# Matrix products without a reader, put at six waits of TensorE in a two-block network

## The chip, the cores and the metric

One core of a Trainium2 chip runs the whole program. Its engines are TensorE (PE, with its weight loads shown apart as PEld), VectorE (DVE), ScalarE (ACT), GpSimd (POOL) and SyncE (SP), which issues the DMAs here. The metric is the device time of one execution in microseconds (us); the time before is the median of three runs.

## The reference

A sequence of 256 tokens of width 1024 passes through four layers and then one more block, all in float32. Each of the four layers has a mixer (Mamba2, HGRN2, a gated delta net, Mamba2 again), a cross attention to 256 memory tokens with four heads, and a gated feed-forward net with a short convolution. The fifth block mixes an RWKV-7 recurrence with a differential attention and ends in a mixture of 32 experts. Cut to what matters here:

```
for i in range(4):
    x = x + mixer_i(rmsnorm(x, ln_mix[i]))            # i = 2: gated delta net
    s = q(x) @ k(mem).T * 256**-0.5                   # 4 heads
    x = x + (softmax(s) @ v(mem)) @ xa_o[i]
    x = x + glu_ffn(rmsnorm(x, ln_ffn[i]))
x = rmsnorm(x, final_norm)                            # passage to the second block
h = rms_norm(x, norm_mix)                             # "mixing"
x = x + (rwkv7(h) and diff_attention(h), gated) @ w_out
x = x + moe(rms_norm(x, norm_ffn))                    # router: top group, top 2 of 8 experts
```

The delta net solves unit triangular systems; the kernel inverts their 32 x 32 diagonal blocks (`base_inverse`) by some thirty steps on VectorE.

## The kernel before

Tokens are kept as two blocks `b` of 128 rows, `x[:, b]`. Every dense product is done in fp32r (a float32 form that PE takes in one pass) on operands split into a high and a low part: three products `l*xh + h*xl + h*xh` into the same PSUM tile (lines 327 to 329, 358 to 360, 395 to 397). ScalarE makes the high part of a weight piece (line 299), VectorE the low one (line 300). Products of plain float32 operands, such as the transposes against the identity (line 188) or against a scaled identity `dg` (line 190), appear in the trace as two records each.

PSUM has eight banks. Four belong to the pool `pm`, tag `m`: each tile of a dense product takes one in turn. The rest belong to a stage's pool `pa` and to the memory's keys and values.

A planner puts the instructions in order before the run. It goes through them with costs of its own and gives each engine the most urgent instruction whose operands are there by its reckoning; urgent is what comes earlier in the program text, and blocks in `high_priority(offset=n)` count as n places earlier. The result is one fixed order for each engine; an engine never steps past an instruction that waits.

The places that the change touches:

- *Begin.* `run` loads `x`, then tables; the tile of the identity and the ones, `id_ones` (trace name `m_ident`), is loaded in `consts`. The first work of PE is the first layer's `norm` (line 194): per token block, squares on ScalarE, `xns = x * gain` on VectorE (line 218), an inverse root by ten short VectorE operations, `dg` (line 234), and then the eight transposes of `transpose_split` (line 190).
- *Passage.* The same `norm`, called from `mix` with `first=final_norm`, does both norms in one; `kept` then holds the two roots of each block, and behind the transposes ScalarE scales `x` (line 237).
- *Last softmax.* `xattn` (line 548) runs for each token block: scores `s` (line 571) for two pairs of heads, maximum, exponentials with sums (line 588), division (line 593), transposes `tp` of the probabilities (line 598) and, after both blocks, the products `po` with the memory's values. `kT` holds the keys, split; `kTh` is its high part. The case `i == 3` is the last of the four.
- *Inverse.* `gdn` calls `base_inverse` (line 997), whose last act is two stream transposes of 128 x 1024 on VectorE (line 1013); the first gives `dT`. The next products of PE there are `pn` (line 1200).
- *Recurrence.* `mix` calls `diff_out` (line 1557): it scales the attention's output `od` by head (line 1563), transposes it (line 1564, `pod`) and splits it (lines 1566 and 1568); behind it stands the RWKV recurrence `wkv`, whose first products are `pA` (lines 1596 and 1597).
- *Router.* `moe` splits the scaled tokens into `hnh` and `hnl` (line 178) while VectorE works out the chosen experts; PE then counts places (`ppos`, lines 1820 to 1824), gathers tokens (`pxe`, line 1887) and starts the experts' first products (`pgu`, line 1917).

Of the kernel before, what the change touches and what calls it, by code (L numbers as in the profile page):

```python
# [11 lines left out]
F32 = mybir.dt.float32  # L12
# [37 lines left out]
class Net:  # L50
# [25 lines left out]
    def consts(self):  # L76
        i = np.arange(128)
        parts = {
            'ident': np.eye(128),
            'ones': np.ones((128, 128)),  # L80
            'neg': np.where(i[:, None] <= i[None, :], 0.0, -1e30),
            'bd32': i[:, None] // 32 == i[None, :] // 32,
            'sub32': np.concatenate([i[:, None] % 32 == i[None, :32],
                                     np.where(i[:, None] % 32 < i[None, :32], 0.0, -1e30),
                                     i[:, None] % 32 < i[None, :32],
                                     i[:, None] // 64 == i[None, :2], np.zeros((128, 30))], axis=1),
            'lin': (i[:, None] <= i[None, :]) * 1.0 - (i[:, None] < 64),
            'lst': (i[:, None] < i[None, :]) * 1.0 - (i[:, None] < 64),
            'blow': i[:, None] // 32 < i[None, :] // 32,
            'tri': i[:, None] <= i[None, :],  # L90
            'stri': i[:, None] < i[None, :],
            'mk3': i[:, None] <= i[None, :],
            'cz': np.zeros((128, 128)),
            'cneg': np.where(i[None, :] <= i[:, None], 0.0, -1e30),
            'tri32': (i[:, None] <= i[None, :]) & (i[:, None] // 32 == i[None, :] // 32),
        }
        self.parts = {k: np.asarray(v, np.float32) for k, v in parts.items()}
        self.c = {}
        self.masks('ident', 'ones', pool=self.const)
        self.ident = self.c['ident']  # L100

    def masks(self, *names, pool=None, **kw):
# [91 lines left out]
    def norm(self, gname, gain, first=None):  # L194
        nc = self.nc
        x = self.x
        g = self.row_table(gname, gain, pool=self.gpool, tag="gain")
        if first is not None:
            gf = self.wpool.tile([128, PIECE], F32, name="wt")[:, :D]
            self.row_load(gf, "final_norm", first)  # L200
        xns = self.wpool.tile([128, 2, D], F32, name="wt")
        hl = self.split_tiles("xn")
        kept = []
        with self.tc.high_priority(offset=NORM):
            for b in range(2):
                xn = xns[:, b]
                ss = self.spool.tile([128, 2, 2], F32, name="ss")
                for n in range(2):
                    s = slice(n * 512, n * 512 + 512)
                    xs = x[:, b, s]  # L210
                    junk = hl[1][:, 4 * n:4 * n + 4, b * 128:b * 128 + 128]
                    sq = lambda k: nc.scalar.activation(junk, xs.rearrange("p (k t) -> p k t", k=4), AF.Square,
                                                        accum_out=ss[:, k, n:n + 1])
                    sq(0)
                    if first is not None:
                        nc.vector.tensor_tensor(xs, xs, gf[:, s], ALU.mult)
                        sq(1)
                    nc.vector.tensor_tensor(xn[:, s], xs, g[:, s], ALU.mult)
                if first is None:
                    m = self.spool.tile([128, 1], F32, name="ssm")  # L220
                    nc.vector.tensor_tensor(m, ss[:, 0, 0:1], ss[:, 0, 1:2], ALU.add)
                    r = self.ms_rsqrt(m, D)
                else:
                    m = self.spool.tile([128, 2], F32, name="ssf")
                    r2 = self.spool.tile([128, 2], F32, name="rsf")
                    nc.vector.tensor_tensor(m, ss[:, :, 0], ss[:, :, 1], ALU.add)
                    nc.vector.tensor_scalar(m, m, KAPPA / D, None, op0=ALU.mult)
                    nc.vector.tensor_scalar(m[:, 0:1], m[:, 0:1], KAPPA * EPS, None, op0=ALU.add)
                    nc.vector.scalar_tensor_tensor(m[:, 1:2], m[:, 0:1], EPS, m[:, 1:2], op0=ALU.mult, op1=ALU.add)
                    self.rsqrt(r2, m)  # L230
                    kept.append(r2)
                    r = r2[:, 1:2]
                dg = self.spool.tile([128, 128], F32, name="dg", bufs=2)
                nc.vector.tensor_scalar(dg, self.ident, r, None, op0=ALU.mult)
                self.transpose_split(hl, xn, b, KD, dg=dg)
        for b, r2 in enumerate(kept):
            nc.scalar.activation(x[:, b], x[:, b], AF.Copy, scale=r2[:, 0:1])
        self.rb = None
        return hl
# [132 lines left out]
    def linear_K(self, src, name, w, kc, tag="ahl", bufs=2):  # L372
        nc = self.nc
        ap = self.dram("in_" + name, pack(w, D))
        ps = [[self.pm.tile([128, 512], F32, name=f"pK{b}{n}", tag="m") for n in range(2)] for b in range(2)]
        for q in range(0, kc, 2):
            ws = self.weights(ap[0][:, q * D:(q + 2) * D], 2 * D)
            if isinstance(tag, str):
                t = self.apool.tile([128, 2, 2, T], F32R, name="ahl", tag=tag, bufs=bufs)
                hl = t[:, 0], t[:, 1]  # L380
            else:
                hl = [self.apool.tile([128, 2, T], F32R, name="ahl", tag=x, bufs=bufs) for x in tag]
            self.split(hl, slice(None), src(q) if callable(src) else src[:, q:q + 2])
            xh, xl = hl
            end = q + 2 == kc
            order = [(k, b, n) for k in range(2) for b in range(2) for n in range(2)]
            if end:
                order.sort(key=lambda x: (x[2], x[1]))
            for k, b, n in order:
                h, l = ws[k]  # L390
                first, last = q + k == 0, q + k == kc - 1
                bs = slice(b * 128, b * 128 + 128)
                c = slice(n * 512, n * 512 + 512)
                p = ps[b][n]
                nc.tensor.matmul(p, xh[:, k, bs], l[:, c], start=first, stop=False)  # L395
                nc.tensor.matmul(p, xl[:, k, bs], h[:, c], start=False, stop=False)  # L396
                self.last_mm = nc.tensor.matmul(p, xh[:, k, bs], h[:, c], start=False, stop=last)  # L397
                if last:
                    self.residual(n, b, p)

    def linear_T(self, *a, **k):
        for f in self.tiles_T(*a, **k):
# [145 lines left out]
    def xattn(self, i):  # L548
# [8 lines left out]
        kT, qT = self.split_tiles("kT", pool=self.apool), self.split_tiles("qT", pool=self.apool)  # L557
# [15 lines left out]
        for b in range(2):  # L573
# [4 lines left out]
            for g in range(2):  # L578
                s = self.pa.tile([128, 2, T], F32, name="s", tag="a")
                for j in range(2):  # L580
                    h = 2 * g + j
# [4 lines left out]
                for j in range(2):  # L586
                    h = 2 * g + j
                    nc.scalar.activation(pr[:, h], s[:, j], AF.Exp, bias=mx[:, h:h + 1], scale=rs[:, b:b + 1],
                                         accum_out=sm[:, h:h + 1])
            rc = self.spool.tile([128, 4], F32, name="rc")  # L590
            nc.vector.reciprocal(rc, sm)
            for h in range(4):
# [8 lines left out]
        for h in range(4):  # L601
            p = self.pa.tile([128, 2, T], F32, name="po", tag="a")
# [34 lines left out]
    def run(self, out):  # L637
        self.x = self.xpool.tile([128, 2, D], F32, name="x")
        ax = self.dram("in_x", self.data['x'].reshape(T, D)).rearrange("(b p) d -> p b d", p=128)
        with self.tc.high_priority(offset=4 * LOAD):  # L640
            for b in range(2):
                self.load(self.x[:, b], ax[:, b])
        self.out = out.rearrange("(b p) d -> p b d", p=128)
        first = [s for s in STAGES if s[:-1] not in ('mix', 'moe')]
        if first:
            self.first_block(first)
# [387 lines left out]
    def gdn(self, i):  # L1034
        nc, d, c = self.nc, self.data, self.c
        w = d['g_in_w'][0]
# [84 lines left out]
        for b in range(2):  # L1121
# [6 lines left out]
            for h in range(8):  # L1128
                for q in range(4):
# [7 lines left out]
                                    pk[:, :, None, :].to_broadcast([128, 8, 2, 32]), ALU.mult)  # L1137
        dT, dD = [x.rearrange("p (b h) i -> p b h i", b=2)
                  for x in self.base_inverse(md.rearrange("p b h i -> p (b h) i"), "inv", 2, reuse=True, xtag="vtok")]
        for b in range(2):  # L1140
            nc.vector.tensor_tensor(dD[:, b], dD[:, b], nb[:, b, :, None].to_broadcast([128, NH, 32]), ALU.mult)
        qT = unit("qT_", 0, 128 ** -0.5)
# [159 lines left out]
    def mix(self, i):  # L1302
# [254 lines left out]
        def diff_out():  # L1557
            odT = [late("odT", [128, 4, T], F32R, tag="o", bufs=2) for _ in range(2)]
            r = self.ms_rsqrt(dss, 128)
            for b in range(2):  # L1560
# [6 lines left out]
                for h in range(4):  # L1567
                    nc.vector.scalar_tensor_tensor(odT[1][:, h, t], pt[:, h], sub[:, 0:1], odT[0][:, h, t].bitcast(F32),
                                                   op0=ALU.mult, op1=ALU.subtract)
            return odT  # L1570


# [185 lines left out]
    def moe(self, i):  # L1758
# [84 lines left out]
        for n in range(2):  # L1843
            for b in range(2):
                self.split_scaled((hnh, hnl), (slice(None), b, slice(n * 512, n * 512 + 512)), parts[b][n], self.r[:, b:b + 1])

        slots = ['xw'] * XW + ['wt'] * 4 + ['hl'] * 3 + ['xnh', 'xnl']
        count = [0]
# [221 lines left out]
```

## Time and profile before

| | |
|---|---|
| median of three runs | 2945.12 us (2937.13 to 2953.91) |
| profiled execution | 2940.76 us, span 2939.0 us |
| mean granted clock of PE | 0.988 |
| busy: PE, DVE, ACT | 2816.4, 1884.7, 1534.5 us |
| DMA | 599.47 MB, mean 204 GB/s |

The span runs from the first instruction to the last; all instants below are counted from its start. The granted clock is 1.00 at 2.4 GHz and 0.50 at 1.2 GHz. Matmuls overlap, so the duration of one is longer than the distance to the next; a pace is read from a count and the time that it took. A line of idle time in brackets says how long the engine stood still before the group, and what released it.

### The profile page before, as it was taken

Reading aid. Unit: us, or ns where it says so; the run is one execution under the profiler, and the core shown is the slowest. Engines: PE = TensorE matmul, PEld = TensorE weight load, DVE = VectorE, ACT = ScalarE, POOL = GpSimd, SP = SyncE. Lnnn points to the kernel's source line nnn. Section 1 sums busy time; section 2 is a strip of 40 time slices with the busy share of each in tenths; the row PEclk is TensorE's granted clock in tenths of the full one; section 3 lists DMA queues with packets and bytes.
Section 4 is the critical chain, followed back from the end, with each engine's and each line's share of the span. In section 5 each row is a group of like instructions: output and inputs, shape, how many; then the busy total and the mean of one; then the engine's idle time right before and its main releaser. Section 6 shows DMA issues by size and latency. Waiting matters only on the chain.

```text
span 2939.0 us, 47392 instructions
## 1 busy us (share of the span) xinstructions
PE 2816.4 (96%) x18834; PEld 2344.3 (80%) x18834; DVE 1884.7 (64%) x3690; ACT 1534.5 (52%) x2870; POOL 5.4 (0%) x19
## 2 busy tenths in 40 slices
PE   8999899999999998999999999989989999999998
PEld 7998899887899897888898999879878785433334
DVE  7886578667678679677786788658769673111103
ACT  7785555555655466675555687545554533111113
POOL 0000000000000000000000000000000000000000
PEclk9999999999999999999999999999999999999999
DMA  5444455552655453235455444535544249999996
GB/s 212 151 158 172 152 197 200 179 189 102 199 187 196 155 179 123 97 120 180 166 200 184 167 150 141 191 122 191 195 155 158 73 178 372 423 422 424 422 423 252
DMA packets 119029, 599.47 MB, mean 204 GB/s; under 512 B 20624, under 2 KB 26769, under 8 KB 56977
## 3 DMA queue, kind: packets, MB, share of 16 engines
q1 hardware_dynamic: 118800, 596.37, 55.1%
q8 instruction: 150, 2.46, 0.3%
q14 instruction: 79, 0.64, 0.1%
HBM read 586.89 MB, written 9.44 MB: 203 GB/s over the span
## 4 chain that ended last, share of the span: by engine, by line
PE 78%; DVE 9%; ACT 7%; DMA 4%; issue 2%; SPq 0%; ACTq 0%; DVEq 0%
PE pT L327 9%; PE pT L329 9%; PE pT L328 9%; PE pgu L1917 7%; PE pK L395 4%; PE pK L396 4%; PE pK L397 4%; PE pM L358 4%; PE pM L359 4%; PE pM L360 4%; PE pyd L1963 3%; PE pkv L538 3%; DVE wl L300 2%; ACT wh L299 1%; DMA kw<-in_xa_v 1%
## 5 line engine op out<-in xcount | busy, mean ns | idle before, releaser
L300 DVE TENSOR_TENSOR wl<-wt,wh 128x1024 fp32r<-128x1024 f32 x620 | 756.4, 1222 | 332.9 <-ACT wh L299 331.7
L299 ACT ACTIVATE wh<-wt 128x1024 fp32r<-128x1024 f32 x620 | 656.3, 1062 | 488.4 <-PE pT L329 234.1
L327 PE MATMUL pT<-xnh,wl 128*128 128x256 f32 x2672 | 746.5, 280 | 4.2 <-DVE wl L300 3.5
L328 PE MATMUL pT<-xnl,wh 128*128 128x256 f32 x2672 | 745.7, 279 | 0.7 <-DVE xnl L174 0.7
L329 PE MATMUL pT<-xnh,wh 128*128 128x256 f32 x2672 | 745.9, 279 | 0.0
L327 PEld LDWEIGHTS pT<-xnh,wl 128*128 128x128 f32 x2672 | 503.5, 189 | 9.0 <-DVE wl L300 5.7
L328 PEld LDWEIGHTS pT<-xnl,wh 128*128 128x128 f32 x2672 | 503.6, 188 | 2.1 <-DVE xnl L174 1.3
L329 PEld LDWEIGHTS pT<-xnh,wh 128*128 128x128 f32 x2672 | 503.8, 189 | 1.9 <-issue 1.3
L396 PE MATMUL pK<-wh,ahl 128*128 128x512 f32 x576 | 230.0, 399 | 0.3 <-DVE ahl L174 0.3
L395 PE MATMUL pK<-wl,ahl 128*128 128x512 f32 x576 | 228.3, 400 | 1.4 <-DVE wl L300 1.0
L397 PE MATMUL pK<-wh,ahl 128*128 128x512 f32 x576 | 229.1, 398 | 0.0
L358 PE MATMUL pM<-wl,xnh 128*128 128x512 f32 (+1 forms) x560 | 194.6, 347 | 1.2 <-ACT xnh L173 1.2
L359 PE MATMUL pM<-wh,xnl 128*128 128x512 f32 (+1 forms) x560 | 193.7, 346 | 0.7 <-DVE xnl L174 0.7
L360 PE MATMUL pM<-wh,xnh 128*128 128x512 f32 (+1 forms) x560 | 192.9, 345 | 0.0
L1917 PE MATMUL pgu<-xw,xe 128*64 128x512 f32 x584 | 148.8, 595 | 0.2 <-DMA xw<-in_w_up 0.2
L510 ACT ACTIVATE kh<-kw,ln_mem 128x256 fp32r<-128x256 f32 x256 | 116.5, 503 | 60.6 <-DMA kw<-in_xa_v 31.3
L511 DVE SCALAR_TENSOR_TENSOR kl<-kw,ln_mem,kh 128x256 fp32r<-128x256 f32 x256 | 114.7, 481 | 36.7 <-ACT kh L510 36.6
L395 PEld LDWEIGHTS pK<-wl,ahl 128*128 128x128 f32 x576 | 108.2, 188 | 29.1 <-DVE wl L300 2.1
L397 PEld LDWEIGHTS pK<-wh,ahl 128*128 128x128 f32 x576 | 108.4, 188 | 25.2
L396 PEld LDWEIGHTS pK<-wh,ahl 128*128 128x128 f32 x576 | 108.4, 188 | 24.9 <-DVE ahl L174 0.5
L179 DVE SCALAR_TENSOR_TENSOR yl<-pyd,ws,y 128x512 fp32r<-128x512 f32 x32 | 24.0, 751 | 149.8 <-ACT y L178 148.0
L358 PEld LDWEIGHTS pM<-wl,xnh 128*128 128x128 f32 x560 | 105.8, 189 | 13.0 <-ACT xnh L173 1.9
(786 smaller groups left out, 5006.3 us busy)
## 6 DMA issues: line engine op xcount, KB each, us to landing
wt<-in_f_up SPq DMA_DIRECT2D x88, 1024.0 KB, 4.9
wt<-in_f_down SPq DMA_DIRECT2D x44, 1024.0 KB, 4.6
xw<-in_w_gate SPq DMA_DIRECT2D x39, 1024.0 KB, 16.0
xw<-in_w_up SPq DMA_DIRECT2D x34, 1024.0 KB, 17.1
wt<-in_m_in_x SPq DMA_DIRECT2D x32, 1024.0 KB, 4.9
xw<-in_w_down SPq DMA_DIRECT2D x26, 1024.0 KB, 17.4
wt<-in_w_down SPq DMA_DIRECT2D x18, 1024.0 KB, 19.6
wt<-in_m_in_z SPq DMA_DIRECT2D x16, 1024.0 KB, 5.0
```

The lines of the kernel that those rows point to most:

```text
L299: nc.scalar.activation(h[:, :m], wt[:, s:s + m], AF.Copy)
L300: nc.vector.tensor_tensor(l[:, :m], wt[:, s:s + m], h[:, :m].bitcast(F32), ALU.subtract)
L327: nc.tensor.matmul(p[:, j], l[:, c], xh[:, k], start=(i == 0 or t > 0 and k == 0), stop=False, skip_group_check=True)
L328: nc.tensor.matmul(p[:, j], h[:, c], xl[:, k], start=False, stop=False, skip_group_check=True)
L329: self.last_mm = nc.tensor.matmul(p[:, j], h[:, c], xh[:, k], start=False, stop=(k == kc - 1), skip_group_check=True)
L358: nc.tensor.matmul(ps[b], xh[:, k, bs], l[:, c], start=(k == 0), stop=False)
L359: nc.tensor.matmul(ps[b], xl[:, k, bs], h[:, c], start=False, stop=False)
L360: self.last_mm = nc.tensor.matmul(ps[b], xh[:, k, bs], h[:, c], start=False, stop=(k == kc - 1))
L395: nc.tensor.matmul(p, xh[:, k, bs], l[:, c], start=first, stop=False)
L396: nc.tensor.matmul(p, xl[:, k, bs], h[:, c], start=False, stop=False)
L397: self.last_mm = nc.tensor.matmul(p, xh[:, k, bs], h[:, c], start=False, stop=last)
L1917: nc.tensor.matmul(p[64 * e:64 * e + 64], xe[kk // 2][:, kk % 2, c], wts[e][k // 2][:, (k % 2) * 512:(k % 2) * 512 + 512], start=(kk == 0) ...
```

## The change

A helper `warm(n, x, w)` takes a fresh tile of `pm` and issues `n` products of a stationary operand `w` (the identity where none is given) with a moving operand `x` into it, each overwriting the last. Nothing reads the tile. It is called at six places: 5 products of 256 columns at the begin, 8 of 512 at the passage (two for each quarter of `xns`), 18 of 256 in each of the two token blocks of the last softmax, 4 of 512 behind the inverse, 2 of 512 at the end of `diff_out`, 12 of 512 in the router. Those with `kT` and `hnh` are fp32r, the others float32. What the program returns is the same.

```
-        self.masks('ident', 'ones', pool=self.const)
+        self.id_ones = self.masks('ident', 'ones', pool=self.const)
...
                 self.transpose_split(hl, xn, b, KD, dg=dg)
+        if kept:
+            for n in range(2):
+                for b in range(2):
+                    self.warm(2, xns[:, b, n * 512:n * 512 + 512])
         for b, r2 in enumerate(kept):
...
+    def warm(self, n, x, w=None):
+        p = self.pm.tile([128, 512], F32, name="warm", tag="m")
+        for _ in range(n):
+            self.nc.tensor.matmul(p[:, :x.shape[-1]], self.ident if w is None else w, x, start=True, stop=True)
...
                                          accum_out=sm[:, h:h + 1])
+            if i == 3:
+                self.warm(18, kT[0][:, 0], kT[0][:, 0, 0:128])
             rc = self.spool.tile([128, 4], F32, name="rc")
...
         self.out = out.rearrange("(b p) d -> p b d", p=128)
+        self.warm(5, self.id_ones)
         first = [s for s in STAGES if s[:-1] not in ('mix', 'moe')]
...
                   for x in self.base_inverse(md.rearrange("p b h i -> p (b h) i"), "inv", 2, reuse=True, xtag="vtok")]
+        self.warm(4, dT[:, 0].rearrange("p h i -> p (h i)"))
...
                                                    op0=ALU.mult, op1=ALU.subtract)
+            self.warm(2, od[:, 1].rearrange("p h k -> p (h k)"))
             return odT
...
                 self.split_scaled((hnh, hnl), (slice(None), b, slice(n * 512, n * 512 + 512)), parts[b][n], self.r[:, b:b + 1])
+        self.warm(12, hnh[:, 1, 512:1024], hnh[:, 1, 512:640])
```

## Rows read from the trace of the kernel before

**Rows 1.** The page: busy us (share) x instructions; DMA tenths in 40 slices.

```profile
PE 2816.4 (96%) x18834; PEld 2344.3 (80%) x18834; DVE 1884.7 (64%) x3690; ACT 1534.5 (52%) x2870; POOL 5.4 (0%) x19
...
DMA  5444455552655453235455444535544249999996
```

**Rows 2.** Windows at half clock: length, busy PE, PEld, DVE, ACT, POOL; clock, DMA, GB/s.

```profile
1156.63:1163.45 6.82, 2.81 (x13) 2.60 (x13) 6.82 (x14) 4.97 (x15) 0.00 (x0) 0.50 0.35 129
1928.03:1931.45 3.42, 3.42 (x19) 3.42 (x18) 2.64 (x5) 2.90 (x5) 0.00 (x0) 0.50 0.03 12
1934.87:1941.69 6.82, 5.08 (x22) 4.71 (x23) 2.70 (x7) 1.80 (x5) 0.00 (x0) 0.50 0.01 2
2160.15:2170.39 10.24, 5.48 (x26) 5.51 (x27) 8.31 (x34) 6.11 (x10) 0.00 (x0) 0.50 0.79 320
2317.15:2327.39 10.24, 9.78 (x30) 7.24 (x31) 6.29 (x9) 4.75 (x12) 0.00 (x0) 0.50 0.29 103
2450.27:2457.11 6.84, 5.54 (x27) 5.44 (x27) 2.72 (x15) 0.85 (x2) 0.00 (x0) 0.50 0.84 349
sum 44.38, PE 32.11 PEld 28.93 DVE 29.48 ACT 21.38 POOL 0.00; mean PE 5.35 PEld 4.82 DVE 4.91 ACT 3.56 POOL 0.00
```

**Rows 3.** Windows, sum over the seven other stretches at half clock.

```profile
sum 23.90, PE 22.80 PEld 22.64 DVE 16.22 ACT 12.44 POOL 0.00; mean PE 3.26 PEld 3.23 DVE 2.32 ACT 1.78 POOL 0.00
```

**Rows 4.** Windows of line 190 on PE: length, busy PE (records), clock, DMA, GB/s.

```profile
10.89:17.10 6.21, 6.21 (x31) 1.00 0.98 378
...
1031.51:1033.33 1.82, 1.82 (x16) 1.00 0.54 108
...
2164.90:2170.39 5.49, 5.48 (x26) 0.50 0.96 400
```

**Rows 5.** The chain that ended last, last softmax: start, us, what.

```profile
1919.22 0.12 PE s L571
...
1920.76 2.76 PE s L571 x23
```

**Rows 6.** Tile `m_ident`: its load, issue in us, and time to landing.

```profile
L111 SPq DMA_DIRECT2D m_ident<-c_ident_ones x1: 432/432/432, 3.8 to 3.8; - x1
...
DMA to landing us min/median/max: 5.5/5.5/5.5
```

**Rows 7.** Timeline of DVE and PE, inverse: start, us, instruction, [idle before].

```profile
1153.74 3.82 DVE L1013 STREAM_TRANSPOSE dd<-X 128x1024 f32<-128x1024 f32 x2
...
1160.64 2.05 PE L1200 MATMUL pn<-dec,bD 128*128 128x128 f32 x8 [6.38 <-issue]
```

**Rows 8.** Timeline of PE, last softmax.

```profile
1926.55 0.93 PE L598 MATMUL tp<-m_ident,prob 128*128 128x128 f32 x6 [3.04 <-DVE prob L593]
...
1936.05 1.94 PE L598 MATMUL tp<-m_ident,prob 128*128 128x128 f32 x8 [3.99 <-DVE prob L593]
```

**Rows 9.** Tile `kTh`, last softmax: durations in ns, first and last start.

```profile
L173 ACT ACTIVATE kTh<-kvraw x2: 1048/1054/1060, 1898.5 to 1899.5; 128x1024 fp32r<-128x1024 f32 x2
```

**Rows 10.** Timeline of DVE and PE, passage.

```profile
2160.39 0.69 DVE L218 TENSOR_TENSOR wt<-x,norm_mix 128x512 f32<-128x512 f32 x1
...
2164.91 6.42 PE L190 MATMUL tp<-dg,wt 128*128 128x128 f32 x32 [9.22 <-DVE rsf L135]
```

**Rows 11.** Timeline of DVE and PE, recurrence.

```profile
2312.45 0.28 DVE L1563 TENSOR_SCALAR od<-od,rs 128x128 f32<-128x128 f32 x1
...
2313.36 0.33 PE L1564 MATMUL pod<-m_ident,od 128*128 128x128 f32 x1
...
2317.61 1.29 PE L1596 MATMUL pA<-ER,bn 64*128 64x256 f32 x3 [2.19 <-DVE odT L1568]
```

**Rows 12.** Timeline of ACT and PE, router.

```profile
2443.85 1.33 ACT L178 ACTIVATE hnh<-xnp,r 128x512 fp32r<-128x512 f32 x2
...
2450.06 0.47 PE L1820 MATMUL ppos<-sel,m_stri 128*128 128x32 f32 x2 [3.84 <-DVE sel L1816]
```

**Rows 13.** Windows, router: as rows 2.

```profile
2457.00:2463.00 6.00, 6.00 (x38) 3.51 (x38) 0.32 (x2) 2.07 (x4) 0.00 (x0) 0.99 0.01 4
```

More of the change, by code (lines that the diff above doesn't have):

```diff
@@ L98, in consts @@
         self.c = {}
-        self.masks('ident', 'ones', pool=self.const)
+        self.id_ones = self.masks('ident', 'ones', pool=self.const)
         self.ident = self.c['ident']
@@ L235, in norm @@
                 self.transpose_split(hl, xn, b, KD, dg=dg)
+        if kept:
+            for n in range(2):
+                for b in range(2):
+                    self.warm(2, xns[:, b, n * 512:n * 512 + 512])
         for b, r2 in enumerate(kept):
@@ L399, in linear_K, with warm @@
                     self.residual(n, b, p)
+    def warm(self, n, x, w=None):
+        p = self.pm.tile([128, 512], F32, name="warm", tag="m")
+        for _ in range(n):
+            self.nc.tensor.matmul(p[:, :x.shape[-1]], self.ident if w is None else w, x, start=True, stop=True)
     def linear_T(self, *a, **k):
@@ L589, in xattn @@
                                          accum_out=sm[:, h:h + 1])
+            if i == 3:
+                self.warm(18, kT[0][:, 0], kT[0][:, 0, 0:128])
             rc = self.spool.tile([128, 4], F32, name="rc")
@@ L643, in run @@
         self.out = out.rearrange("(b p) d -> p b d", p=128)
+        self.warm(5, self.id_ones)
         first = [s for s in STAGES if s[:-1] not in ('mix', 'moe')]
@@ L1139, in gdn @@
                   for x in self.base_inverse(md.rearrange("p b h i -> p (b h) i"), "inv", 2, reuse=True, xtag="vtok")]
+        self.warm(4, dT[:, 0].rearrange("p h i -> p (h i)"))
         for b in range(2):
@@ L1569, in diff_out @@
                                                    op0=ALU.mult, op1=ALU.subtract)
+            self.warm(2, od[:, 1].rearrange("p h k -> p (h k)"))
             return odT
@@ L1845, in moe @@
                 self.split_scaled((hnh, hnl), (slice(None), b, slice(n * 512, n * 512 + 512)), parts[b][n], self.r[:, b:b + 1])
+        self.warm(12, hnh[:, 1, 512:1024], hnh[:, 1, 512:640])
         slots = ['xw'] * XW + ['wt'] * 4 + ['hl'] * 3 + ['xnh', 'xnl']
```

## The prediction

> **What bounds the kernel now.** I read the page's busy shares first [rows 1]: TensorE (PE) is busy for 96% of the span, the other engines far less. So nearly every microsecond that leaves PE's own stream, or the few waits in it, leaves the time. The exception is the end: from the 34th of 40 slices on (2425 us) the DMA engines stand at nine tenths or more, and there PE follows the weights. Next I looked for stretches in which PE's clock is granted at 0.50 (1.2 instead of 2.4 GHz), by stretches cut at the edges of the clock. There are thirteen while PE works. Six lie at five of the named places (the inverse, twice at the last softmax, the passage, the recurrence, the router) and hold 32.11 us of PE work [rows 2]; seven lie elsewhere (three near 303 to 348 us, then 798, 1122, 1914, 2218) and hold 22.80 us, which nothing in the change touches [rows 3]. Work at 1.2 GHz takes twice as long, so the change can regain at most half of 32.11, 16.1 us, and the begin.
>
> At the begin the granted clock reads 1.00, but the pace says otherwise. At 1031 us 16 records (8 products of 128 f32 columns, two records each) take 1.82 us, 0.23 us a product. At the passage 26 records at 0.50 take 5.49 us, 0.42 us a product. The begin has 31 records in 6.21 us, 0.40 us a product [rows 4]. So it ran at half for nearly all its transposes, and I trust the pace.
>
> **What is added, and its price.** 67 products, no reader, no DMA; each group takes one buffer of the four in `pm`. Prices go by columns: an f32 product of 256 columns 0.46 us at the full clock and 0.84 at half, of 512 columns 0.92 and 1.68; an fp32r product of 256 columns 0.12 us (23 in 2.76 us [rows 5]), of 512 columns 0.24. The groups cost at the full clock: begin 5 x 0.46 = 2.3, inverse 4 x 0.92 = 3.7, softmax 2 x 18 x 0.12 = 4.3, passage 8 x 0.92 = 7.4, recurrence 2 x 0.92 = 1.8, router 12 x 0.24 = 2.9; 22.4 us in all, twice that at half. They cost nothing only where PE has no other work. PE takes its instructions in a fixed order, so the question at each place is when the operand is there, when PE's last real work ends, and when the next can start.
>
> *Begin.* The identity's load is issued at 3.8 us and lands 5.5 us later, at 9.3 [rows 6]. Five products at half end at 13.5; the transposes, which start at 10.89, then start 2.6 us late. If all 16 then run at the full clock (3.7 us), they end at 17.2, as now. If the products themselves were already at the full clock, 15.3: 2 us gained. If nothing is faster, 2.6 us lost. At the passage PE worked for 5.5 us before the clock rose; counted from 9.3 that is 14.8, with 3 transposes done and 13 left at 0.23: 17.8. I take 0.5 us late, from that nearest row, and keep -2 to +2.6.
>
> *Inverse.* The operand is the first of two stream transposes, 3.82 us together, done at about 1155.65. PE's last real product ends at 1154.3 and the next starts at 1160.64 after 6.38 us [rows 7]. Four products end at 1159.4: covered. At half (if the clock had fallen first) they would end at 1162.4, 1.7 us late. The gain: 2.81 us of work at half [rows 2], 1.4 at most; DVE is busy in all 6.82 us of that stretch, so I take 1.0.
>
> *Last softmax.* The two waits are 3.04 and 3.99 us [rows 8]. The operand, `kTh`, is written at 1898.5 to 1900.6 [rows 9], long before, so nothing but the planner's order of readiness holds the 36 products back. The scores `s` of the first heads hang on the same keys and are more urgent, yet the first of them stands at 1919.22 [rows 5], some 19 us after the keys: the planner had no hole before that, so none for the new ones either. Both groups then fall largely in the first wait: 25 of the 36 fit into 3.04 us; 11 go on, up to 1.3 us late, or stand in the second wait, 1.3 of 3.99 us, too little to count on. So I count the first stretch (3.42 us of work, 1.7 gained) less a late start of 1.0: 0.7 us. The bounds: both stretches regained (8.50 / 2 = 4.25 us), and 4.3 us lost if all 36 stand ahead of work that is ready.
>
> *Passage.* PE waits for 9.22 us, until 2164.91. Its operands come in quarters, the last at 2161.08 [rows 10]. Eight products at 0.92 from where PE stops, 2155.69, reach 2163.1, and two behind the last quarter 2162.9: covered. They start where PE has just stopped, at the full clock. The gain is half of 5.48, 2.7 us. All at half they would end at 2169.1, 4.2 us late.
>
> *Recurrence.* The last scaled `od` is there at 2312.73. The two products, behind the last transpose of `od` (2313.69), end at 2315.5; what stands between that and the start of the wait, 2315.42, moves by 1.8 us and ends at 2317.3; the wait, 2.19 us, ends at 2317.61 [rows 11]: covered, by 0.3 us. The gain is at most half of 9.78, 4.9 us. DVE is busy in 6.29 and ACT in 4.75 of these 10.24 us [rows 2], so some of it would wait for DVE's products; I take 4.0. The lower bound is 0, the other 1.7 us lost, if the products run at half.
>
> *Router.* The operand is there at 2445.2 and PE's `pM` end at 2446.2; twelve products end at 2449.1, before `ppos` at 2450.06 [rows 12]: covered. Half of 5.54 is 2.8; some DVE work between `ppos` and the gathering stays. I take 2.5 us, with bounds 0 and 2.8. It does reach the end: from 2457 to 2463 us the DMA share is 0.01 [rows 13], the buffers being full until PE eats the first weights, so an earlier PE restarts the stream that sets the end.
>
> **Sum.** +0.5 - 1.0 - 0.7 - 2.7 - 4.0 - 2.5 = -10.4 us. The profiled execution took 2940.76 us (span 2939.0), which gives 2930.4. It lies 4.4 us below the median of the three runs, 2945.12; against that the sum is 2934.7, and I forecast **2935 us** (0.35% less).
>
> **A rule weighed.** The rows tell one execution's stretches of half clock. The Trainium skill, page "TensorE: Matmul & The Clock Gate", Part 1, says that where the clock turns is not fixed to the kernel's start and differs from run to run, and that for modelling the ramp's penalty is under 1% of a typical span. By the size the trace agrees (half of 32.11 + 22.80 is 27.5 us, 0.93% of the span); no row here can show the differing from run to run.
>
> **The rivals.**
> - *All the half clock at these places goes.* For it: at five of the six the products start where PE has just stopped or end close to the next work. Against it: the second softmax wait, and DVE's share at the inverse and the recurrence. 16.1 us and up to 2 at the begin: 18.1, a time of 2927.
> - *The clock falls, or the waiting hides it anyway.* Either the products are not enough to hold the clock over the rest of each wait (1.4 us ahead and 1.2 behind at the inverse, 1.9 at the passage, 1.0 at the router), or the shorter products only make PE wait for DVE. Against it: 6.38 and 9.22 us of standing still shrink to 2.6 and 1.9. Gain 0 to 5 us: 2942.
> - *The stretches do not repeat.* The thirteen are those of one execution. If the clock's turns fall elsewhere in the next, a wait that cost here need not cost there, above all a short one (2.19 and 3.04 us), and others may; without the 4.0 and 0.7 us of these two the gain is 5.7 us: 2939. The rule just named speaks for it. Against it, the long waits (6.38, 9.22) would cost in any execution.
> - *Slower: the planner's order.* PE's queue cannot step past the new products, and the planner places them by its own reckoning of what is ready. If it puts them ahead of work that on the chip is ready, they cost their own time, 22.4 us at the full clock if none is covered (2967.5), and keep no clock up in the waits. It decides against the change once more than 10.4 us of them, about half, stand outside waits: with half, and nothing regained, 2956. For it: the keys and the identity are there early. Against it: every operand but these two is made inside the wait itself, and these two groups cost 4.3 and 2.6 us at most.
> - *It does not do what it says* (products moved elsewhere or left out, the same time): part of the second.
>
> **Chances.** The forecast 0.52 (its own range 2930 to 2940), everything regained 0.18, nothing or little 0.14, stretches that do not repeat 0.11, slower 0.05. Less than 0.5% either way (14.7 us) is what a measurement of this kernel cannot tell from no change. Faster by more: 0.15 from the second case and 0.14 from the upper part of the first, 0.29. Slower by more: most of the last, 0.04. The rest, 0.67, is within. The range runs from 2921, everything regained and 6 us of the 8 by which the lowest run lies under the median, to 2949, nothing regained and 4 us over it, which leaves out most of the slower case.
>
> **What would show it.** Right: the granted clock stays at 1.00 from 2155 to 2175 and from 2312 to 2330; the 32 records of the passage take about 3.7 us and not 6.4; `pn` at the inverse takes about 1.05 us and not 2.05; `pgu` starts 2.5 us sooner behind `ppos`; the new products stand inside the idle time of before. Wrong: half-clock rows at the same places; transposes at the begin that end later than 18.5; products of the softmax between query products; or gaps of DVE that take the place of PE's. A time under 2925 or over 2950 would say that something besides these waits has moved.

## The result, and the profile after

The changed kernel takes **2976.42 us** (median of six runs, 2975.09 to 2982.45). The kernel before, run on the same chip, takes 2945.05 (six runs, 2937.13 to 2953.91). The ratio is 1.0106, with a 95% interval from 1.0083 to 1.0129: 31 us slower, where I forecast 10 us faster. The profiled execution took 2980.92 us, 40 us more than the one of before (2940.76); some 8 of these 40 lie in two stages that run slower in some executions, whatever the change (last section).

The page first: PE's line of busy time, to be held against [rows 1].

```profile
span 2979.1 us, 47595 instructions
...
PE 2852.6 (96%) x18920; PEld 2365.2 (79%) x18920; DVE 1891.9 (64%) x3690; ACT 1537.3 (52%) x2870; POOL 5.5 (0%) x19
```

PE is busy 36.2 us more than before, and it waits 126.5 us of the span where it waited 122.6 (2939.0 - 2816.4). The new products fill 26 us of PE over all six groups, yet in sum the waits did not shrink: where a group filled one, others grew elsewhere. By this sum alone the loss could be the products' own price; the experiments show that it is not. The clock won nothing either. This is the last line of the windows over the fourteen stretches that stand at half clock now:

```profile
sum 61.20, PE 55.29; mean PE 3.95
```

55.3 us of PE's work stand at half clock, before it was 32.11 + 22.80 = 54.9 [rows 2, 3].

**Where the time went in.** I took instructions that both traces have, the first of a name in a stage, and the time by which it starts later after the change:

```
first                     starts before   later by
pT, behind the begin          17.18        -0.8
pd, ahead of the inverse    1089.12         1.1
pn, behind the inverse      1160.64        41.7
pK, end of the delta net    1287.05        44.8
tp, last attention          1870.72        52.8
s, its scores               1919.06        35.4
tp, passage                 2164.91        36.5
pdo, ahead of recurrence    2286.43        35.7
psm, behind recurrence      2438.81        40.8
tp, end                     2904.42        39.8
```

Most of it comes at one of the six places, the inverse (+43.7 from `pd` to `pK`); 17.5 come back at the last attention; the recurrence adds 5.1. The 8.0 between `pK` and the last attention hold one of the slow stages of the last section (4.2). Two views show what happened. First PE's timeline around the products of the inverse:

```profile
1137.31 0.41 PE L548 MATMUL pkv<-mnl,kh 128*128 128x256 f32 x1
1137.52 4.19 PE L409 MATMUL warm<-dd,m_ident 128*128 128x512 f32 x8
1141.14 0.68 PE L331 MATMUL pT<-xnh,wl 128*128 128x256 f32 x1
...
1202.29 1.13 PE L1214 MATMUL pn<-dec,bD 128*128 128x128 f32 x8 [0.22 <-ACT wh L303]
```

The first transposed block, the operand, is there at 1136.1 (1155.8 before), because DVE had less besides the inverse to do: 14 us of work for `pkv` in place of 31 us for the projections (`wl`, `cv`). But `pn` comes at 1202 (1160 before), since the projections that PE had not done now stand between the two. The second view is windows of PE, for one tile alone: length, busy PE (records), clock, DMA share, GB/s. The `pT` products of the q projection, before, from `pd` to `pn`:

```profile
1089.12:1160.64 71.52, 28.73 (x237) 0.95 0.38 132
```

and after, from `pd` to the new products:

```profile
1090.26:1137.72 47.46, 0.00 (x0) 0.87 0.34 112
```

Before, the projections ran on PE while DVE inverted. After, not one `pT` stands there: they all wait behind the new products, and begin with the record after them. PE did the memory products `pkv` of later layers in their place. Windows of `pkv` before, cut at the instructions of the table:

```profile
1089.12:1287.05 197.93, 18.56 (x123) 0.97 0.33 112
1287.05:1629.79 342.74, 31.62 (x233) 1.00 0.49 169
1629.79:1870.72 240.93, 13.04 (x91) 1.00 0.46 158
1870.72:1919.06 48.34, 19.99 (x137) 0.96 0.57 202
```

and after:

```profile
1090.26:1331.87 241.61, 42.19 (x256) 0.97 0.34 117
1331.87:1681.06 349.19, 31.94 (x221) 1.00 0.47 166
1681.06:1923.53 242.47, 7.00 (x48) 0.99 0.42 147
1923.53:1954.42 30.89, 0.00 (x0) 0.94 0.64 232
```

The 43.7 us from `pd` to `pK` are 23.6 us of `pkv` drawn forward, 4.2 us of new products, and 16.7 us of other work, less 0.8 of waits. The other work is above all 149 `pT` that before had stood ahead of `pd`; in their place ahead of `pd` stand 11 us more of `pkv` (144.1 where 132.9 were). So `pkv` are a loan of 35 us, and only half comes back: 20 us are missing where the last attention begins, and that stretch is 17.5 us shorter. The 6 us missing from the third stretch bring nothing: it is 1.5 us longer, PE's waits in it grew from 1.9 to 5.5 us (length less busy time), and 3.4 us of its work stand at half clock, where none did. Another 7.5 us are lost in the `pkv` themselves: the same 1536 products take 225.2 us in all where they took 217.7. Between `pd` and `pK` 12.2 us of PE's work stand at half clock, 5.8 before.

At the recurrence the same thing happens on a smaller scale. PE's timeline after, to be held against [rows 11]:

```profile
2342.73 2.78 PE L1578 MATMUL pod<-m_ident,od 128*128 128x128 f32 x7 [5.77 <-DVE od L1577]
2346.80 1.19 PE L1611 MATMUL pA<-ER,bn 64*128 64x256 f32 x2 [1.29 <-DVE itmp L1020]
...
2348.18 3.00 PE L409 MATMUL warm<-od,m_ident 128*128 128x512 f32 x4
```

Before, PE did `pM` products up to `pod` and waited for nothing there. Now it stands for 5.77 and 1.29 us, and pays for the same `pM` behind the recurrence: ahead of the first `tp` there, 21 before and 69 after, 16 us in place of 5.

### The profile page after: what moved, and what is told of

Its sections match the earlier page's. It is cut to its first block, busy times and chain, and to the rows that moved or that the text cites. A ratio compares the mean times of both kernels' runs of the same rounds, so it can differ in the third digit from the quotient of the medians.

```text
span 2979.1 us, 47595 instructions
## 1 busy us (share of the span) xinstructions
PE 2852.6 (96%) x18920; PEld 2365.2 (79%) x18920; DVE 1891.9 (64%) x3690; ACT 1537.3 (52%) x2870; POOL 5.5 (0%) x19
## 4 chain that ended last, share of the span: by engine, by line
PE 77%; DVE 10%; ACT 6%; DMA 6%; issue 2%; SPq 0%; ACTq 0%; DVEq 0%
PE pT L331 9%; PE pT L332 9%; PE pT L333 9%; PE pgu L1933 7%; PE pK L399 4%; PE pK L400 4%; PE pK L401 4%; PE pM L364 4%; PE pM L362 4%; PE pM L363 4%; PE pyd L1979 3%; PE pkv L548 3%; DVE wl L304 2%; DMA kw<-in_xa_k 1%; DMA kw<-in_xa_v 1%
```

## The experiments

**Theory R (the ring).** Each group writes a tile of its own out of the four banks of `pm`. The planner hands the banks of a ring out in the order of the program, at the turn of a tile's first writer. So no product that writes a later `pm` tile (`pT`, `pM`, `pK`, `pv`) can stand ahead of the group, and the group waits for its operand: the work that filled the wait is locked behind it. **Theory P (the price):** the 26 us of products simply cost what they take. **Theory C (the clock):** half-clock stretches move, 1.7 us each.

I could count part of R in the order of PE's instructions as built, from the last `pk` to the first `pn`:

```
                          ahead of the new products      behind them
                          pT    pM    pkv                pT    pM    pkv
before                    235   48    68                 -     -     -
inverse alone             0     0     199                332   48    18
bank alone                0     0     199                332   48    21
bank opened early         231   48    51                 2     0     0
```

What the order costs was for the chip to say. All the ratios below are against the kernel before on the same chip.

**Inverse alone.**

```diff
+        self.warm(4, dT[:, 0].rearrange("p h i -> p (h i)"))
```

> Only the four products at the inverse are left of the change. Theory R (the ring): the tile that they write is asked for from the ring of four pm banks in program order, the planner hands no later pm bank out before it, so the products of the q, v and z projections, which stood in the 50 us of DVE's inverse, stand behind it; memory products pkv are drawn forward in their place and are missing later. In the trace of the whole change pn (behind the inverse) is 40.6 us later by what it had lost to the transposes before it, and 18 us of that come back by the last attention's scores, where the pkv that stood there are gone; so this group alone should cost 30 to 40 us: 2975 to 2985 us. Theory P (the price): the products cost what they take, 4 us, and this kernel takes 2945 to 2950. Theory C (the clock): the half-clock stretches move, each is worth 1.7 us, so within 2940 to 2952.

Measured: 2976.79 us, ratio 1.0101 (1.0058 to 1.0144), 30 us slower. One group of four products makes the greater part of the loss, or all of it: 17 us at the interval's lower end. P and C are out by far.

**The bank alone.**

```diff
-        self.warm(4, dT[:, 0].rearrange("p h i -> p (h i)"))
+        self.warm(1, dT[:, 0, 0, 0:1])
```

> At the inverse one product of one column, into a tile of its own from pm, in place of four of 512 columns: the request for the bank stays, the work goes. R: nearly the same loss as with the four products, 26 to 36 us (2971 to 2981), since the order is nearly the same (no pT before it, 199 pkv before it in place of 68). P: nothing, 2943 to 2947. C: like P, or a few us to either side.

Measured: 2973.32 us, ratio 1.0096 (1.0060 to 1.0132), 28 us slower. The work of the products is not the cause; the request is. (The group stands two lines lower in the program than in the change, behind the scaling of `dD`; so it does in the next experiment.) PE's timeline shows the lock open:

```profile
1126.81 0.58 PE L405 MATMUL warm<-dd,m_ident 128*128 128x1 f32 x2 [1.36 <-DVE dd L1019]
1127.26 0.56 PE L327 MATMUL pT<-xnh,wl 128*128 128x256 f32 x1
```

PE stood 1.36 us for `dd`, did one product of one column, and from the next record on the projections ran.

**The bank opened early.**

```diff
+        p = self.pm.tile([128, 512], F32, name="warm", tag="m")
+        self.warm(1, self.ident[:, 0:1], p=p)
+        self.warm(4, dT[:, 0].rearrange("p h i -> p (h i)"), p=p)
```

> The four products at the inverse, into a pm tile whose first writer is one product of one column with an operand that is there from the start (the identity), so that the bank is handed out at once and the ring goes on with the three others; the four products themselves still wait for the inverse. R: most of the loss goes, because the projections stand before the inverse again (231 pT records before it, as 235 before the change): 2943 to 2952, some us for three banks in place of four. P: like the inverse alone, about 2949. If the loss came from the bank being held for so long (a want of banks and not the order of the ring), it would stay: over 2965.

Measured: 2947.21 us, ratio 0.9997 (0.9967 to 1.0028): the loss is gone, with the same four products and a bank held through the whole inverse. So it is the order in which banks are handed out, not a want of banks. The group's place in the program is not what saves it: in "Opened early, without the softmax" it stands exactly where the change has it, and the loss is gone too. PE's timeline at the wait, against [rows 7]:

```profile
1157.99 3.70 PE L405 MATMUL warm<-dd,m_ident 128*128 128x512 f32 x8 [0.86 <-DVE dd L1019]
...
1162.85 1.13 PE L1209 MATMUL pn<-dec,bD 128*128 128x128 f32 x8 [0.92 <-issue]
```

Here the step that I had forecast is seen: four products in 3.70 us inside the wait, and `pn` at the full clock, 1.13 us where it took 2.05. It won no time that can be measured: from `pd` to `pK` this trace is 0.5 us longer than that of before. A stretch at half clock ahead of the wait, 3.4 us long before (at 1122), is 6.8 us long here (at 1125).

**No bank at all.** The products write the tile of `pn`, which the real products overwrite.

```diff
             pn = self.pa.tile([128, 4, 128], F32, name="pn", tag="a")
+            if g == b == 0:
+                self.warm(4, dT[:, 0].rearrange("p h i -> p (h i)"), p=pn.rearrange("p a b -> p (a b)"))
```

> The same four products at the inverse, written into the pn tile that the next real products overwrite: no bank of the pm ring. R: no loss, 2941 to 2947, and pn at the full clock as in the forecast (1 us gained there). P: 4 us lost, 2949. C: within some us of before.

Measured: 2953.40 us, ratio 1.0014 (0.9995 to 1.0033). The 30 us are gone, as R says, and PE's order from the last `pk` to `pn` is that of before (235 `pT`, 48 `pM`, 68 `pkv`). Between nothing and the 4 us of P the runs cannot tell; in the trace the way from `pd` to `pK` is 3.2 us longer.

**All but the inverse.** The change without its line at the inverse.

> The whole change without the group at the inverse: begin, softmax, passage, recurrence and router as changed. Theory R (a pm bank asked for in program order keeps later pm work behind the products): the loss of 31 us goes nearly all; by the shifts between the same instructions in the two traces, begin -0.9, softmax +1.2, passage -2.5, recurrence +6.6, router -1.0, so +3.4: 2945 to 2952. Theory P (the products' own price, 26 us of PE records in the trace of the change, 4 of them at the inverse): 2968 to 2974, the loss less the 4 us of this group.

Measured: 2953.90 us, ratio 1.0028 (1.0013 to 1.0043), 8 us slower: above what I expected, and a third of the price theory. With the 30 us of the inverse it makes 38; the whole change makes 31 (24 to 38). Its trace puts the loss at the recurrence: from `pdo` to `psm` it is 7.8 us longer than before, with the wait of 5.8 us at `pod` and 17.1 us at half clock (10.2 before).

**Recurrence alone.**

```diff
+            self.warm(2, od[:, 1].rearrange("p h k -> p (h k)"))
             return odT
```

> Only the two products at the recurrence. R: in the order, 42 pM products that stood between pdo and the first pA stand behind the products, so PE waits for od with nothing to do (5.8 us in the trace of the change) and pays for the pM later: the stretch from the last pdo to the first psm of the routed part gets longer by 5 to 8 us, the kernel by as much (2950 to 2957). P: 2 us at most. Forecast: 4 us shorter.

Measured: 2951.08 us, ratio 1.0022 (1.0010 to 1.0035), 6.5 us slower; from the last `pdo` to `psm` the trace is 6.0 us longer. The wait is the one of the whole change:

```profile
2317.84 2.71 PE L1570 MATMUL pod<-m_ident,od 128*128 128x128 f32 x7 [5.71 <-DVE od L1569]
```

**Recurrence, bank opened early.**

```diff
+            p = self.pm.tile([128, 512], F32, name="warm", tag="m")
+            self.warm(1, self.ident[:, 0:1], p=p)
+            self.warm(2, od[:, 1].rearrange("p h k -> p (h k)"), p=p)
             return odT
```

> The same two products, into a pm tile that one product of one column of the identity opens early. R: the 42 pM products stand before pod again, the wait at pod goes, and the stretch to psm is not longer than before; with the clock held as forecast it is up to 4 us shorter: 2941 to 2946. P: like the recurrence alone. If holding one of four banks costs pM its pairs, it is some us longer.

Measured: 2936.96 us, ratio 0.9970 (0.9950 to 0.9990): faster than before, by 3 to 15 us. The stretch from `pdo` to `psm` is 4.2 us shorter. PE's timeline, and the window in which the clock had been at half:

```profile
2330.16 1.88 PE L406 MATMUL warm<-od,m_ident 128*128 128x512 f32 x4
...
2334.19 0.67 PE L1606 MATMUL pA<-ER,bn 64*128 64x256 f32 x2 [0.39 <-DVE odT L1575]
```

```profile
2328.78:2339.02 10.24, 9.85 (x43) 5.82 (x41) 10.24 (x17) 7.64 (x20) 0.00 (x0) 1.00 0.00 0
```

Two products in 1.88 us; the wait of 2.19 us [rows 11] is 0.39; the clock is 1.00 throughout.

**Opened early, without the softmax.** Begin, passage and router as changed, inverse and recurrence with the bank opened early.

> The change without the softmax group, with the banks at the inverse and at the recurrence opened early. R: no stretch longer than before by more than 2 us; begin -0.9, inverse 0 to -1, passage -2.5, recurrence 0 to -4, router -1.0: 4 to 9 us less, 2936 to 2942, a ratio of 0.997 to 0.9985 that the runs can hardly tell from 1. P: 15 us more or so, 2960. C (the half-clock stretches only move, and do not get fewer): within 2 us of before.

Measured: 2941.16 us, ratio 1.0000 (0.9987 to 1.0013), by the medians 3 us less. The loss of 31 us is gone with the locks; of the hoped 4 to 9 us nothing is certain.

**Control of the recurrence.** As with the bank opened early, but the two products have one column.

```diff
-            self.warm(2, od[:, 1].rearrange("p h k -> p (h k)"), p=p)
+            self.warm(2, od[:, 1, 0, 0:1], p=p)
```

> The control of the recurrence with the bank opened early: the same tile and the same order of everything else, but its two products have one column in place of 512, so they cannot hold the clock. If the clock is what that kernel wins by: the stretch 2312 to 2330 stands at half again, nothing is won between the last pdo and psm (that kernel: 4.2 us), 2941 to 2947. If the changed order of the pM products wins: 4 us less as there, 2937 to 2941.

Measured: 2953.57 us, ratio 0.9998 (0.9982 to 1.0013). PE's order there is that of the kernel with the bank opened early, but for the two small products, which stand some 3 us earlier. The stretch from `pdo` to `psm` is 0.3 us longer than before, and the half clock is back:

```profile
2333.00:2343.40 10.40, 9.90 (x30) 7.37 (x31) 6.33 (x9) 4.74 (x12) 0.00 (x0) 0.51 0.29 102
```

So it is the products' work in the wait that holds the clock, and the clock that wins the 4.2 us. It is the one step of the forecast that is shown in full, and it needed the lock open.

**Four sites.** Begin, passage and router as changed, the recurrence opened early.

> Begin, passage and router as changed, the recurrence with its bank opened early, nothing at the inverse and the softmax. Theory R with the shifts read so far: begin -0.7, passage -0.5 (2.3 at the transposes, nearly all given back by pdo), recurrence -4.2, router -0.5: 5 to 6 us less, 2937 to 2941. If the forecast's steps held in full (passage -2.7, router -2.5): 10 us less, 2934.

Measured: 2948.75 us, ratio 0.9985 (0.9969 to 1.0001), 4 us less; `pdo` to `psm` again 4.3 us shorter.

**Begin, passage and router.**

> Begin, passage and router alone, as changed. R: 1 to 2 us less, no difference that the runs can tell, 2941 to 2946. Forecast: begin +0.5, passage -2.7, router -2.5, 2940. Price theory: their 15 us of products show, 2955 or more.

Measured: 2943.67 us, ratio 0.9965 (0.9952 to 0.9977): 10 us faster, more than I expected and without any product at the recurrence; yet the stretch from `pdo` to `psm` is 6.2 us shorter. In the order of this kernel 16 `pM` and not 4 stand behind the second `pA`, in the recurrence's wait.

**Passage alone.**

```diff
+        if kept:
+            for n in range(2):
+                for b in range(2):
+                    self.warm(2, xns[:, b, n * 512:n * 512 + 512])
```

> Only the eight products at the passage, as changed. In the order of this kernel 16 pM products and not 4 stand in the recurrence's wait behind the second pA, as in the kernel with begin, passage and router, where the half-clock stretch there was gone and the stretch from the last pdo to psm 6.2 us shorter. If that order is what won there: the same here, 5 to 7 us in that stretch and 0 to 2 from the transposes to pdo, so 6 to 9 us less in all (2936 to 2939 where before takes 2945). If begin or router won it: nothing between pdo and psm, and 0 to 2 us in all.

Measured: 2937.29 us, ratio 0.9973 (0.9960 to 0.9986), 8 us faster, as expected of the order. `pdo` to `psm` is 6.1 us shorter, with the clock at full:

```profile
2312.70:2328.00 15.30, 14.54 (x67) 10.24 (x66) 13.70 (x20) 10.40 (x26) 0.00 (x0) 1.00 0.29 101
```

The products at the passage moved the planner's reckoning, and twelve more real `pM` fell into a wait 150 us later. The clock stays at full there as with the new products, and the twelve are work that had to be done anyway: 6.1 us against 4.2. That it is these twelve that hold it is read from the order of two kernels (this one and the one before it); no run takes them out again. That gain is real but was not designed. Begin, passage and router (0.9965), the recurrence opened early (0.9970) and passage alone (0.9973) are the versions that beat both kernels, and their intervals overlap.

## Why the prediction was wrong

The forecast was 2935 us, the range 2921 to 2949, the chance of slower by more than 0.5% 0.04. The step that failed is the one for each place, "covered": I compared when the operand is there with when PE's work ends in the trace of before, and took PE's other work to stay where it was. The text named the buffer ("each group takes one buffer of the four in `pm`") and priced it at nothing. In its place the runs showed that PE's other work does not stay: the request alone, with one column of work, costs 28 us at the inverse. By place:

- *Begin*, +0.5 (-2 to +2.6; its own working, 17.8 against 17.10, gives 0.7): four of the ten records stand ahead of the transposes, four between and two behind them, and the transposes end at 16.32 (17.10 before). From the first `tp` to the first `pT` the five traces with the group take 1.1 us less to 0.4 more than before, the eight without it 1.3 less to 0.3 more: nothing that can be told.
- *Inverse*, -1.0: +30 alone. With the lock open the step itself came true (3.70 us covered, `pn` 1.13 us), and was worth nothing measurable. The sign that I had set, `pn` at 1.05 us, is met in the changed kernel too (1.13, 1202.29), where it says nothing: a right sign can stand in a stage that lost 40 us.
- *Last softmax*, -0.7: six records between the last query products and the scores, close to the sign that I had set for wrong (between query products), and thirty in the first wait:

```profile
1953.70 0.88 PE L409 MATMUL warm<-kTh 128*128 128x256 f32 x6
...
1957.30 3.76 PE L409 MATMUL warm<-kTh 128*128 128x256 f32 x30
```

From `s` to the first `po` it is 1.2 us longer than before, and 0.2 to 1.4 in the experiments, with the group or without: about nothing.
- *Passage*, -2.7: right in its mechanism. PE's timeline, against [rows 10]:

```profile
2192.27 7.51 PE L409 MATMUL warm<-wt,m_ident 128*128 128x512 f32 x16
2201.36 4.03 PE L190 MATMUL tp<-dg,wt 128*128 128x128 f32 x32 [1.57 <-DVE dg L234]
```

Eight products in 7.51 us (7.4 forecast), the transposes in 4.03 us (3.7 forecast, 6.42 before), 2.3 us gained at `pT`. But at `pdo`, 115 us on, 0.8 of it are left, and between -0.3 and 1.5 in the five experiments with the group. PE's waits for DVE in between grew by 0.6 us only (2.9 after, 2.3 before), so the second rival, shorter products that wait for DVE, covers a part; where the rest went I cannot say, since the order of `pT` there changed too.
- *Recurrence*, -4.0: +5.1 in the changed kernel, +6.0 alone; -4.2 once the bank is opened early. The size was right, the cover was not: I took "what stands between" to move by 1.8 us, and it could not stay ahead.
- *Router*, -2.5: from `ppos` to the end it is 1.0 us shorter, and 0.1 to 1.1 in the four experiments with the group, where those without it lie between 0.3 shorter and 0.7 longer: a gain of half a microsecond or so. The products end at 2489.73, two waits are left, and the half clock came again:

```profile
2490.85 0.41 PE L1835 MATMUL ppos<-sel,m_stri 128*128 128x32 f32 x2 [1.12 <-DVE sel L1831]
...
2493.48 0.93 PE L1903 MATMUL pxe<-oh,hnl 128*128 128x256 f32 x4 [1.30 <-DVE oh L1892]
```

```profile
2493.80:2497.20 3.40, 3.40 (x19) 0.50 0.76 313
```

The prices of single products were right. The rival "planner's order" had the right place, the planner, and the wrong mechanism: not products ahead of ready work that cost their own time (22.4 us at most), but a request that keeps ready work back, at any length of the products. That is why one column costs 28 us, and why the rival's price and its chance were both too small. The rival "the stretches do not repeat" is not borne out at the named waits (last section). What stays open is how the 30 us of the inverse divide between longer waits, half clock and work done later: the stretches were followed in the trace of the whole change alone.

## What to carry to other kernels

Before adding an instruction that nobody reads, ask what it takes besides its engine's time: a tile out of a rotating pool, asked for in program order, can lock in all later users of that pool until the tile's first writer may run. Look in the trace for what fills a wait's neighbourhood now and which pool it writes, and compare the order of the two programs stage by stage, not only at the places of the change. At the recurrence real work moved into the wait gained more (6.1 us) than products that nobody reads (4.2). If a wait has to be filled with such products, open their tile early or let them write a tile that is needed next: both take the lock away, and neither won time at the inverse.

## What was not expected of the hardware

**Two paces of the same products.** In the four feed-forward stages PE is busy without a gap and the granted clock reads 1.00; yet in some executions a stage takes 4.2 us more. Groups of instructions of PE from 425 to 455 us (records, busy us, mean ns of one), before:

```profile
L327 PE MATMUL pT<-xnh,wl 128*128 128x256 f32 x89 | 24.6, 276 | 0.0
```

and with the recurrence opened early, which has the same order up to there:

```profile
L327 PE MATMUL pT<-xnh,wl 128*128 128x256 f32 x86 | 24.2, 281 | 0.0
```

89 records against 86 in 30 us. There is nothing between the two paces: where 1056 `pT` of such a stage follow each other, they take 122.2 or 122.3 us, or else 126.4 to 126.7, in all fourteen traces. The profiled execution of before has no slow stage, that of the changed kernel two (8 us of its 40), and that of the recurrence opened early four (17 us), by which it is the slowest of its ten runs (2952.93, median 2936.96). I found no cause. Four slow stages would be enough for the spread of before's six runs (2937.13 to 2953.91), but only profiled executions have a trace, so this is not shown. It is a reason not to compare one profiled execution with another by its span.

**The half clock comes back at the same places.** The kernel with the recurrence opened early has PE's order of before up to the last `pdo`, and these windows stand at half:

```profile
1131.05:1137.85 6.80, 6.08 (x18) 5.18 (x19) 6.80 (x27) 2.39 (x6) 0.00 (x0) 0.50 0.10 39
1168.60:1175.40 6.80, 4.41 (x20) 4.20 (x21) 5.80 (x14) 4.91 (x15) 0.00 (x0) 0.50 0.20 72
```

By their instants they seem to be others than the one of [rows 2], 1156.63 to 1163.45. But this execution is 10.4 us behind there (`pn` at 1170.99, 1160.64 before): the second is the wait ahead of `pn` again, begun 1.6 us later against `pn`, and the first is the stretch that before has at 1122, twice as long. So it is in the four traces with this order (before, recurrence alone, opened early, and its control): held against PE's instructions, the half clock stands within 3 us of the same places: at the inverse, twice at the last softmax, at the passage, and near 324, 344, 799 and 1122 us of before. What differs are lengths (3.4 or 6.8 us at 1122 and at the first of the softmax) and a few short stretches (303, 711, 1914, 2218). The prediction cited the Trainium skill, page "TensorE: Matmul & The Clock Gate", Part 1, for the gate's turns differing from run to run, and said that no row could show it. These traces agree for the lengths and the short stretches, not for the waits: there the clock fell each time. What no execution promises is that a stretch won at one wait is not lost at the next: with its lock opened, the inverse's wait kept its clock, and the stretch ahead of it was twice as long.
